# Block inverses of the gated DeltaNet mixer: from ten steps over pairs of heads to five steps over fours

## Chip, core and metric

The kernel runs on one core of a Trainium2 chip. The metric is device time in microseconds (us) of one execution. The kernel before takes 1231.0 us, the median of three runs (1230.87 to 1231.64).

## What is computed

A decoder trunk of two layers over 512 tokens of width 1024, all in float32. Layer 0 mixes tokens with gated linear attention, layer 1 with a gated DeltaNet; each is followed by a gated ConvFFN, and each sublayer by a LayerNorm. The change lies in the DeltaNet of layer 1, which has 8 heads:

```python
m = jnp.where(strict, jnp.einsum('bhnik,bhnjk->bhnij', k_beta, k) * decay_ij, 0.0)
rhs = jnp.concatenate([v * beta[..., None], k_beta * jnp.exp(bcum)[..., None]], axis=-1)
sol = lax.linalg.triangular_solve(m, rhs, left_side=True, lower=True, unit_diagonal=True)
...
def step(state, inp):
    qk_n, u_n, w_n, qd_n, kd_n, cd_n = inp
    v_new = u_n - jnp.einsum('bhck,bhkv->bhcv', w_n, state)
    o_n = jnp.einsum('bhck,bhkv->bhcv', qd_n, state) + jnp.einsum('bhij,bhjv->bhiv', qk_n, v_new)
    state = state * cd_n[..., None, None] + jnp.einsum('bhck,bhcv->bhkv', kd_n, v_new)
    return state, o_n
```

The kernel works on blocks of 128 tokens, so each head has four 128x128 unit lower triangular matrices, and it forms their inverses instead of solving.

## The kernel before

**The large work.** Almost all of the program is projections: 128x512 matmuls of float32 split in a high and a low part (xh, xl against wh, wl), three products each. In the DeltaNet (`gdn`) they come as 24 column projections `fm` of 24 such matmuls (k, v, q of eight heads), then as the gate projection `tm` (192 of them), then the output projection. A list of tasks (Python generators) is run beside them: `pump`, called after every few large matmuls, resumes each task whose due time on a rough clock (`clk`) has come. That only sets the order in which the program is written; the scheduler beneath may move an instruction ahead of others that wait for data, and every engine then executes its queue in the order that results.

**The inverses.** VectorE inverts the 32x32 diagonal blocks of all heads at once (`base`). They pass through DRAM (`dinv`, `dinvt`) and come back by small DMAs on the queues of SP and GpSimd into `T` (transposed inverses, one tile for a pair of heads) and `rm` (the result, one tile for a head). TensorE then joins blocks, 32 to 64 (`quarter`) and 64 to 128 (`half`). Each join has two products: V = A·T into one PSUM bank, copied to SBUF, then R = T'·V, copied into `rm`; `am` is A. In `quarter` both 64-blocks of a matrix are joined, the products being 32x32: V at rows 0-31 and output partitions 32-63 (n=0) and at rows 64-95 and 96-127 (n=1), R at rows 32-63 and 0-31 and at rows 96-127 and 64-95; one more product, R at rows 32-63 and 32-63, gives the transposed block that the half join needs, copied into `T`. So there are five places in TensorE's array, five tiles of it. In `half` the products are 64x64, V at rows 0-63 and partitions 64-127, R at rows 64-127 and 0-63: two tiles. A pair of heads has eight matrices, so one join of a pair has 8 products at each place. Every float32 product is executed as two passes, and the trace counts passes.

`inverses` goes over pairs: step `quarter(k)` writes the V products of pair k beside the R products of pair k-1, and `half(k)` likewise. Ten steps; `block_turn` holds them `INV_APART` = 3.2 us of that rough clock apart, and the first comes `INV_DELAY` = 18 after the first pair's DMAs are issued:

```python
for step, k in ((quarter, 0), (quarter, 1), (quarter, 2), (half, 0), (quarter, 3), (half, 1), (quarter, 4),
                (half, 2), (half, 3), (half, 4)):
    yield from self.block_turn(INV_APART)
    step(k)
```

`block_turn` also ties the first product of a step behind the last 128x512 matmul written before it (`behind`), so a step does not start earlier.

**What follows.** `chain(g)` runs the recurrence of heads 4g to 4g+3 over the four blocks of tokens, 128x128 products named vn, kT, qs, s, o, ks, with `tm` matmuls between; it needs `rm` of its four heads. q's last two heads have transposes qT and products pq, which are among the steps too. After the chains the gates are applied, transposed (yT), and the output projection follows.

Of the kernel before, what the change touches and what calls it, by code (L numbers as in the profile page):

```python
# [46 lines left out]
LOOKAHEAD = 2  # L47
TAIL = 4
HEADSTART = 4
INV_DELAY = 18.0  # L50
INV_APART = 3.2
CONV_DELAY = 6.0
V_DELAY = 18.0
COLS_DELAY = 64.0
# [8 lines left out]
def c4(t):  # L63
    return t.rearrange("p (c i) -> p c i", c=4)


def blk(i, n=P):
    return slice(i * n, i * n + n)


class Trunk:
# [1386 lines left out]
    def gdn(self, li, g, b):  # L1458
        nc = self.nc
# [11 lines left out]
        q, k, v, am, rm, pj = ([None] * DH for _ in range(6))  # L1471
# [131 lines left out]
        def base():  # L1603
# [17 lines left out]
            for pair in range(4):  # L1621
                t = self.slot("T")
                t8 = t.rearrange("p (u i) -> p u i", u=8)
                nc.gpsimd.memset(t8[:32, :, 32:], 0.0)
                for hd in (2 * pair, 2 * pair + 1):
                    rm[hd] = self.slot("rm")
                    nc.gpsimd.memset(rm[hd], 0.0)
                for qq in range(4):
                    rw = blk(qq, 32)
                    u = pair // 2 * 64 + qq * 16 + pair % 2 * 8  # L1630
                    if qq < 3:
                        nc.sync.dma_start(t8[rw, :, blk(qq % 2, 32)],
                                          self.dinvt[u:u + 8].rearrange("u i c -> i u c"))
# [11 lines left out]
        parts = []  # L1645

        def inverses():

            low, up = slice(0, 32), slice(32, 64)
            units = [(i, ck, 4 * i + ck) for i in range(2) for ck in range(4)]
            views = {}

            def views_of(pair):
                if pair not in views:
                    both = (2 * pair, 2 * pair + 1)
                    views[pair] = ([c4(am[hd]) for hd in both], [c4(rm[hd]) for hd in both], parts[pair], self.slot("V"))
                return views[pair]

            def quarter(k):
                if k < 4:
                    a, _, t8, vs = views_of(k)
                    pv = [self.psum("V") for _ in range(2)]
                if k > 0:
                    _, r, t0, v0 = views_of(k - 1)
                    pr = [self.psum("R") for _ in range(2)]
                for i, ck, u in units:
                    w = blk(u, 32)
                    for n, o in ((0, 0), (1, 64)):  # L1670
                        m = slice(o + 32, o + 64)
                        if k < 4:
                            self.mm(pv[n][m, w], a[i][o:o + 32, ck, m], t8[o:o + 32, u, low])
                        if k > 0:
                            self.mm(pr[n][o:o + 32, w], v0[m, w], r[i][m, ck, m])
                    if k > 0:
                        self.mm(pr[0][up, w], r[i][up, ck, up], v0[up, w])
                if k < 4:
                    nc.scalar.copy(vs[up, :256], pv[0][up, :256])
                    nc.vector.tensor_copy(vs[96:, :256], pv[1][96:, :256])  # L1680
                if k > 0:
                    nc.scalar.copy(t0[up, :, low], pr[0][up, :256].rearrange("p (u i) -> p u i", u=8))
                    for n, o in enumerate((0, 64)):
                        for i in range(2):
                            nc.vector.tensor_copy(r[i][o:o + 32, :, o + 32:o + 64],
                                                  pr[n][o:o + 32, blk(i)].rearrange("p (c i) -> p c i", c=4))

            def half(k):
                if k < 4:
                    a, _, t8, vs = views_of(k)  # L1690
                    pv = self.psum("V")
                if k > 0:
                    _, r, _, v0 = views_of(k - 1)
                    pr = self.psum("R")
                for i, ck, u in units:
                    w = blk(u, 64)
                    if k < 4:
# [3 lines left out]
                if k < 4:  # L1701
                    nc.scalar.copy(vs[64:, :], pv[64:, :])
                if k > 0:
                    for i in range(2):
                        nc.vector.tensor_copy(r[i][:64, :, 64:], pr[:64, blk(i, 256)].rearrange("p (c i) -> p c i", c=4))
                        am[2 * k - 2 + i] = None
                        self.set(("rm", 2 * k - 2 + i), 1.0)
# [229 lines left out]
```

## Time and profile before

| | before |
|---|---|
| runs, median (lowest to highest) | 1231.0 us (1230.87 to 1231.64) |
| the profiled execution | 1231.2 us |
| its span, first to last instruction | 1229.5 us |
| granted TensorE clock | 0.999 |
| steps of the inverses on TensorE | 719.8 to 755.0 us of the span |
| V and R products, passes | 192 of V, 256 of R (320 of 32x32, 128 of 64x64) |

The profile comes from one execution. PE is TensorE, DVE VectorE, ACT ScalarE, POOL GpSimd, and SP issues most DMAs. The chain of waits follows the program back from its last instruction to whatever released each step, so its rows add up to the span; in the timeline a row is a run of like instructions with its start, its length and its count, and a TensorE row's length holds the last matmul's own latency, so that rows overlap by it.

### The profile page before, as it was taken

What the parts mean: (1) busy time and instruction counts of PE and PEld (TensorE: products, weight loads), DVE (VectorE), ACT (ScalarE), POOL (GpSimd) and SP (SyncE); (2) the same over time, 40 slices, a digit from 0 to 9 for tenths busy, and PEclk for the clock granted to TensorE, in tenths of its full rate; (3) what the DMA queues carried; (4) which work ended last, traced back from release to release, by engine and by line L of the source; (5) the groups of instructions that cost most, each with busy time, mean ns of one, the idle gap of its engine ahead of it and who ended that gap; (6) DMA issues with size and microseconds to landing.
All of it is one profiled execution on the core that took longest, in us unless ns stands there. A gap on an engine that the chain in (4) does not pass through costs nothing.

```text
span 1229.5 us, 17177 instructions
## 1 busy us (share of the span) xinstructions
PE 1218.9 (99%) x6546; PEld 1028.8 (84%) x6546; DVE 933.8 (76%) x1533; ACT 605.6 (49%) x1068; POOL 122.6 (10%) x159
## 2 busy tenths in 40 slices
PE   9999999999999999999999999999999999999997
PEld 8888888988888888888988888988988888888886
DVE  4966986689957895666779975688589966796667
ACT  5644764544434443454678555644644434443440
POOL 4000000081000000001152030200053000000000
PEclk9999999999999999999999999999999999999999
DMA  7332353442453123333344351234352263223311
GB/s 213 112 103 69 87 173 101 148 127 72 136 152 99 56 66 113 113 105 104 102 131 129 101 135 37 85 122 138 120 154 69 73 201 89 88 81 103 110 62 69
DMA packets 171042, 133.67 MB, mean 109 GB/s; under 512 B 16374, under 2 KB 140090, under 8 KB 170960
## 3 DMA queue, kind: packets, MB, share of 16 engines
q1 hardware_dynamic: 165888, 123.62, 33.8%
q0 software_dynamic: 3872, 8.30, 2.2%
q8 instruction: 51, 0.84, 0.3%
q10 hardware_dynamic: 1200, 0.66, 0.2%
q14 instruction: 31, 0.25, 0.1%
HBM read 126.77 MB, written 5.78 MB: 108 GB/s over the span
## 4 chain that ended last, share of the span: by engine, by line
PE 96%; DVE 2%; DMA 1%; issue 0%; ACT 0%; DVEq 0%; SPq 0%; ACTq 0%
PE fm L203 54%; PE tm L203 20%; PE fold L203 13%; PE o L203 1%; PE xT L220 1%; PE pq L203 1%; PE pg L203 1%; PE vn L203 1%; PE V L203 0%; PE yT L220 0%; PE s L203 0%; PE qs L203 0%; PE ks L203 0%; DVE wl L649 0%; DMA h<-in_x_dram 0%
## 5 line engine op out<-in xcount | busy, mean ns | idle before, releaser
L203 PE MATMUL fm<-xh,wh 128*128 128x512 f32 (+2 forms) x1104 | 401.8, 366 | 0.7 <-ACT xh L649 0.7
L203 PE MATMUL fm<-xl,wh 128*128 128x512 f32 (+2 forms) x1104 | 399.9, 365 | 0.0
L203 PE MATMUL fm<-xh,wl 128*128 128x512 f32 (+1 forms) x1080 | 392.8, 366 | 0.0
L649 DVE TENSOR_TENSOR wl<-raw,wh 128x1024 fp32r<-128x1024 f32 (+1 forms) x162 | 201.0, 1243 | 152.5 <-ACT wh L649 151.9
L649 ACT CAST wh<-raw 128x1024 fp32r<-128x1024 f32 (+1 forms) x163 | 169.2, 1040 | 224.3 <-PE fm L203 142.1
L203 PEld LDWEIGHTS fm<-xh,wh 128*128 128x128 f32 (+1 forms) x1104 | 206.9, 188 | 33.8 <-ACT xh L649 0.9
L203 PEld LDWEIGHTS fm<-xl,wh 128*128 128x128 f32 (+1 forms) x1104 | 207.0, 188 | 32.5
L203 PEld LDWEIGHTS fm<-xh,wl 128*128 128x128 f32 x1080 | 202.8, 189 | 33.0
L922 DVE SCALAR_TENSOR_TENSOR conv<-fm,ffn_cw,conv 128x511 f32<-128x511 f32 x112 | 83.5, 746 | 8.4 <-ACT conv L920 7.0
L203 PE MATMUL fold<-wh,fh 128*128 128x512 f32 x224 | 87.7, 391 | 0.0
L203 PE MATMUL fold<-wl,fh 128*128 128x512 f32 x224 | 87.4, 390 | 0.1
L203 PE MATMUL fold<-wh,fl 128*128 128x512 f32 x224 | 87.2, 389 | 0.0
L649 ACT CAST wh<-b 128x1024 fp32r<-128x1024 f32 x48 | 49.7, 1055 | 60.3 <-PE fold L203 25.7
L940 ACT ACTIVATE conv<-conv 128x512 f32<-128x512 f32 x44 | 27.9, 634 | 80.4 <-DVE conv L922 80.4
L849 POOL TENSOR_TENSOR h<-h,gb 128x512 f32<-128x512 f32 x16 | 27.4, 1738 | 335.4 <-DMA gb<-in_ln_g_dram 229.6
L649 DVE TENSOR_TENSOR wl<-b,wh 128x1024 fp32r<-128x1024 f32 x48 | 58.0, 1224 | 2.3 <-ACT wh L649 2.3
L1453 DVE SCALAR_TENSOR_TENSOR conv<-fm,gdn_cw,conv 128x511 f32<-128x511 f32 (+2 forms) x72 | 54.0, 790 | 3.2 <-ACT conv L1451 2.6
L203 PE MATMUL tm<-wh,xh 128*128 128x512 f32 x128 | 52.9, 414 | 0.0
L203 PEld LDWEIGHTS fold<-wh,fh 128*128 128x128 f32 x224 | 42.0, 188 | 9.9 <-DVE h L1011 1.2
L203 PE MATMUL tm<-wh,xl 128*128 128x512 f32 x128 | 50.2, 392 | 0.0
L203 PE MATMUL tm<-wl,xh 128*128 128x512 f32 x128 | 50.1, 391 | 0.0
L203 PEld LDWEIGHTS fold<-wl,fh 128*128 128x128 f32 x224 | 42.0, 188 | 9.4 <-DVE wl L649 0.9
(348 smaller groups left out, 1960.3 us busy)
## 6 DMA issues: line engine op xcount, KB each, us to landing
raw<-in_ffn_w_in_dram SPq DMA_DIRECT2D x88, 512.0 KB, 3.9
raw<-in_gdn_w_in_dram SPq DMA_DIRECT2D x32, 512.0 KB, 4.1
raw<-in_ffn_w_out_dram SPq DMA_DIRECT2D x28, 512.0 KB, 3.7
raw<-in_gla_w_in_dram SPq DMA_DIRECT2D x26, 512.0 KB, 3.6
b<-in_ffn_w_out_dram SPq DMA_DIRECT2D x24, 512.0 KB, 4.8
raw<-in_gla_w_out_dram SPq DMA_DIRECT2D x8, 512.0 KB, 4.0
raw<-in_gdn_w_out_dram SPq DMA_DIRECT2D x8, 512.0 KB, 3.9
h<-in_x_dram SPq DMA_DIRECT2D x8, 256.0 KB, 4.3
```

The costliest lines, as they stand in the source:

```text
L203: t = self.nc.tensor.matmul(out, a, b, start=start, stop=stop, skip_group_check=joined)
L220: t = self.nc.tensor.transpose(out, a, self.ident[:n, :n])
L649: return self.nc.scalar.copy(dst_h, src), self.nc.vector.tensor_sub(dst_l, src, dst_h)
L849: nc.gpsimd.tensor_mul(h[hf], h[hf], gb[hf])
L922: nc.vector.scalar_tensor_tensor(a[:, d:], ps[:, :S - d], tap(2 - d), a[:, d:], ALU.mult, ALU.add)
L940: nc.scalar.activation(a, a, AF.Gelu)
L1453: self.conv = nc.vector.scalar_tensor_tensor(a[:, d:], ps[:, :S - d], tap(3 - d), a[:, d:], ALU.mult, ALU.add)
```

## The change

The pairs become fours. `quarter(k)` writes the V products of four k beside the R products of four k-1, and the same in `half`, so there are three calls of each, twice as large; the second bank of V and R that `quarter` already had is filled to 512 columns, and `half` takes two banks for each. The copies out of PSUM double with them. `quarter(2)` and `half(0)` share a step, so five steps are left; they stand 5.4 apart on the rough clock, the first at 20.0 after the DMAs.

```diff
-INV_DELAY = 18.0
-INV_APART = 3.2
+INV_DELAY = 20.0
+INV_APART = 5.4
...
-            units = [(i, ck, 4 * i + ck) for i in range(2) for ck in range(4)]
+            units = [(i, ck, 4 * i + ck) for i in range(4) for ck in range(4)]
...
             def quarter(k):
-                if k < 4:
-                    a, _, t8, vs = views_of(k)
+                if k < 2:
+                    a, _, t, (vs, _) = views_of(k)
                     pv = [self.psum("V") for _ in range(2)]
...
                     for n, o in ((0, 0), (1, 64)):
                         m = slice(o + 32, o + 64)
-                        if k < 4:
-                            self.mm(pv[n][m, w], a[i][o:o + 32, ck, m], t8[o:o + 32, u, low])
+                        if k < 2:
+                            self.mm(pv[n][m, w], a[i][o:o + 32, ck, m], t[i // 2][o:o + 32, u % 8, low])
...
-                if k < 4:
-                    nc.scalar.copy(vs[up, :256], pv[0][up, :256])
-                    nc.vector.tensor_copy(vs[96:, :256], pv[1][96:, :256])
+                if k < 2:
+                    nc.scalar.copy(vs[up, :], pv[0][up, :])
+                    nc.vector.tensor_copy(vs[96:, :], pv[1][96:, :])
...
                 for i, ck, u in units:
-                    w = blk(u, 64)
-                    if k < 4:
-                        self.mm(pv[64:, w], a[i][:64, ck, 64:], t8[:64, u, :])
+                    n, w = u // 8, blk(u % 8, 64)
+                    if k < 2:
+                        self.mm(pv[n][64:, w], a[i][:64, ck, 64:], t[n][:64, u % 8, :])
                     if k > 0:
-                        self.mm(pr[:64, w], v0[64:, w], r[i][64:, ck, 64:])
...
+                        self.mm(pr[n][:64, w], v0[n][64:, w], r[i][64:, ck, 64:])
...
-            for step, k in ((quarter, 0), (quarter, 1), (quarter, 2), (half, 0), (quarter, 3), (half, 1), (quarter, 4),
-                            (half, 2), (half, 3), (half, 4)):
+            for steps in (((quarter, 0),), ((quarter, 1),), ((quarter, 2), (half, 0)), ((half, 1),), ((half, 2),)):
                 yield from self.block_turn(INV_APART)
-                step(k)
+                for step, k in steps:
+                    step(k)
                 yield 0.1
```

What the scheduler makes of it on TensorE is not the five steps as written. In the rows below V_ and R_ are PSUM banks, T_6237, T_6291, T_6363 and T_6417 the inverses of pairs 0 to 3, am and rm the matrices of single heads, and a row stands for one product or for as many as its x says.

First place: TensorE where the inverses begin. Before, the step ends after the products of pair 0 on its two places:

```order
L203 MATMUL V_6447<-T_6237,am_5205 32x32
L203 MATMUL V_6448<-T_6237,am_5205 32x32
L220 MATMUL qT_6467<-ident_86,conv_6308 128x128 x4
L220 MATMUL qT_6476<-ident_86,conv_6392 128x128 x4
L203 MATMUL pq_6485<-conv_6308,conv_5282 128x128 x4
L203 MATMUL pq_6491<-conv_6392,conv_5319 128x128 x4
```

Now the products of pair 1 follow, one place after the other:

```order
L203 MATMUL V_6467<-T_6237,am_5205 32x32
L203 MATMUL V_6468<-T_6237,am_5205 32x32
L203 MATMUL V_6467<-T_6291,am_5255 32x32 x4
L203 MATMUL V_6467<-T_6291,am_5264 32x32 x4
L220 MATMUL qT_6503<-ident_86,conv_6308 128x128 x4
L220 MATMUL qT_6512<-ident_86,conv_6392 128x128 x4
L203 MATMUL pq_6521<-conv_6308,conv_5282 128x128 x2
L203 MATMUL V_6468<-T_6291,am_5255 32x32 x4
L203 MATMUL V_6468<-T_6291,am_5264 32x32 x4
L203 MATMUL pq_6521<-conv_6308,conv_5282 128x128 x2
```

The V products of the second bank for pair 1 have moved between the pq products; the first step is entered twice.

Second place: TensorE in the second step. Before, the five places take turns:

```order
L203 MATMUL V_6517<-T_6291,am_5255 32x32
L203 MATMUL R_6519<-rm_6239,V_6446 32x32
L203 MATMUL V_6518<-T_6291,am_5255 32x32
L203 MATMUL R_6520<-rm_6239,V_6446 32x32
L203 MATMUL R_6519<-V_6446,rm_6239 32x32
```

Now three places take turns eight times, then two (seven times, for heads 2 and 3), then the other two eight times, then one alone; the V products of pair 3 are not in this step at all:

```order
L203 MATMUL V_6541<-T_6363,am_5410 32x32
L203 MATMUL R_6543<-rm_6239,V_6465 32x32
L203 MATMUL R_6543<-V_6465,rm_6239 32x32
...
L203 MATMUL R_6543<-rm_6293,V_6465 32x32
L203 MATMUL R_6543<-V_6465,rm_6293 32x32
...
L203 MATMUL V_6542<-T_6363,am_5410 32x32
L203 MATMUL R_6544<-rm_6239,V_6465 32x32
...
L203 MATMUL R_6544<-rm_6293,V_6465 32x32 x4
L203 MATMUL R_6544<-rm_6295,V_6465 32x32 x3
```

What was written as one turn of five places has been pulled apart into four stretches.

Third place: TensorE in the 64x64 products. Before, V and R of a step take turns between large matmuls:

```order
L203 MATMUL tm_6655<-wh_6400,xl 128x512
L203 MATMUL V_6728<-T_6291,am_5255 64x64
L203 MATMUL R_6729<-rm_6239,V_6446 64x64
L203 MATMUL V_6728<-T_6291,am_5264 64x64
L203 MATMUL R_6729<-rm_6241,V_6446 64x64
L220 MATMUL qT_6749<-ident_86,conv_6497 128x128 x4
```

Now, from the last 32x32 products on (R_6644 is the second bank of the R products of the second four, V_6703 and V_6704 the V products of the first four, V_6729 and V_6730 those of the second, R_6731 and R_6732 the R products of the first):

```order
L203 MATMUL V_6542<-T_6417,am_5595 32x32 x4
L203 MATMUL R_6643<-V_6539,rm_6421 32x32
L203 MATMUL fm_6458<-xl,wh_6316 128x512
L203 MATMUL fm_6458<-xh,wl_6317 128x512
L203 MATMUL R_6644<-rm_6365,V_6539 32x32 x4
...
L203 MATMUL V_6703<-T_6237,am_5196 64x64 x4
...
L203 MATMUL V_6729<-T_6363,am_5419 64x64 x4
L203 MATMUL R_6731<-rm_6239,V_6465 64x64 x4
L203 MATMUL R_6731<-rm_6241,V_6465 64x64 x4
L203 MATMUL V_6730<-T_6417,am_5586 64x64
L203 MATMUL R_6732<-rm_6293,V_6466 64x64
```

24 V products stand in a row, then 8 R products in a row, and only the last 8 of each take turns. The steps three and four have grown together; two large matmuls separate them from the products before.

Counted over the whole stretch, TensorE goes to the small products ten times before (one step each) and seven times now:

| | products in their order, per place (R' is the extra R product) | behind it |
|---|---|---|
| A | V on two places by turns, 8 each; then V on one place, 8 | 8 qT, 2 pq |
| B | V on one place, 8 | 6 pq, 6 fm |
| C | V, R, R' by turns, 8 each; R, R' by turns, 7 and 6; V, R on the other places by turns, 8 each; R alone, 7; R' 2, R 1 each | 6 fm |
| D | V on one place, 8 | 4 fm |
| E | R, R' by turns, 16 and 15; V on one place, 8; R' 1 | 2 fm |
| F | R on one place, 16; then 64x64: V 24, R 8, V and R by turns, 8 each | 6 tm, 4 vn, 4 kT |
| G | 64x64: R 16 | 6 tm |

Before, the ten visits have in their order: V by turns on two places, 8 each; all five places by turns, 8 each; three places by turns, about 6 each, two by turns, about 5, then all five for the rest (the third visit); 64x64 V 8; five places by turns, 8 each; 64x64 V and R by turns, 8 each; R and R' on three places by turns, 8 each; 64x64 V and R by turns, 8 each, twice; 64x64 R 8. The queues of SP and GpSimd issue the DMAs of T and rm in the same order as before. Behind the seventh visit the program holds the same instructions as before, with chain 0 and chain 1 begun earlier among the `tm` matmuls: 42 `tm` now stand between the last o product of the chains and the first yT, and before it was 12.

More of the change, by code (lines that the diff above doesn't have):

```diff
@@ L1651, in inverses, with views_of @@
             low, up = slice(0, 32), slice(32, 64)
-            units = [(i, ck, 4 * i + ck) for i in range(2) for ck in range(4)]
+            units = [(i, ck, 4 * i + ck) for i in range(4) for ck in range(4)]
             views = {}
[L1655 to L1659, printed above, removed]
+            def views_of(four):
+                if four not in views:
+                    heads = range(4 * four, 4 * four + 4)
+                    views[four] = ([c4(am[hd]) for hd in heads], [c4(rm[hd]) for hd in heads],
+                                   parts[2 * four:2 * four + 2], [self.slot("V") for _ in range(2)])
+                return views[four]
             def quarter(k):
-                if k < 4:
-                    a, _, t8, vs = views_of(k)
+                if k < 2:
+                    a, _, t, (vs, _) = views_of(k)
                     pv = [self.psum("V") for _ in range(2)]
                 if k > 0:
-                    _, r, t0, v0 = views_of(k - 1)
+                    _, r, t0, (v0, _) = views_of(k - 1)
                     pr = [self.psum("R") for _ in range(2)]
@@ L1677, in quarter @@
                         self.mm(pr[0][up, w], r[i][up, ck, up], v0[up, w])
-                if k < 4:
-                    nc.scalar.copy(vs[up, :256], pv[0][up, :256])
-                    nc.vector.tensor_copy(vs[96:, :256], pv[1][96:, :256])
+                if k < 2:
+                    nc.scalar.copy(vs[up, :], pv[0][up, :])
+                    nc.vector.tensor_copy(vs[96:, :], pv[1][96:, :])
                 if k > 0:
-                    nc.scalar.copy(t0[up, :, low], pr[0][up, :256].rearrange("p (u i) -> p u i", u=8))
+                    for i in range(2):
+                        nc.scalar.copy(t0[i][up, :, low],
+                                       pr[0][up, blk(i, 256)].rearrange("p (u i) -> p u i", u=8))
                     for n, o in enumerate((0, 64)):
-                        for i in range(2):
+                        for i in range(4):
                             nc.vector.tensor_copy(r[i][o:o + 32, :, o + 32:o + 64],
@@ L1688, in half @@
             def half(k):
[L1689 to L1691 removed]
+                if k < 2:
+                    a, _, t, vs = views_of(k)
+                    pv = [self.psum("V") for _ in range(2)]
                 if k > 0:
                     _, r, _, v0 = views_of(k - 1)
[L1694 removed]
+                    pr = [self.psum("R") for _ in range(2)]
                 for i, ck, u in units:
[L1696 to L1698 removed]
+                    n, w = u // 8, blk(u % 8, 64)
+                    if k < 2:
+                        self.mm(pv[n][64:, w], a[i][:64, ck, 64:], t[n][:64, u % 8, :])
                     if k > 0:
[L1700 to L1702 removed]
+                        self.mm(pr[n][:64, w], v0[n][64:, w], r[i][64:, ck, 64:])
+                if k < 2:
+                    nc.scalar.copy(vs[0][64:, :], pv[0][64:, :])
+                    nc.scalar.copy(vs[1][64:, :], pv[1][64:, :])
                 if k > 0:
[L1704 to L1707, printed above, removed]
[L1709 to L1710 removed]
+                    for i in range(4):
+                        nc.vector.tensor_copy(r[i][:64, :, 64:],
+                                              pr[i // 2][:64, blk(i % 2, 256)].rearrange("p (c i) -> p c i", c=4))
+                        am[4 * k - 4 + i] = None
+                        self.set(("rm", 4 * k - 4 + i), 1.0)
+            for steps in (((quarter, 0),), ((quarter, 1),), ((quarter, 2), (half, 0)), ((half, 1),), ((half, 2),)):
                 yield from self.block_turn(INV_APART)
[L1712 removed]
+                for step, k in steps:
+                    step(k)
                 yield 0.1
```

## The prediction, made before the changed kernel was run

> **What bounds the kernel now.** I read the busy times first, then what TensorE waited for, then the chain of waits through the stretch that is changed, then the timeline of TensorE inside the visits.
>
> ```profile
> PE 1218.9 (99%) x6546; PEld 1028.8 (84%) x6546; DVE 933.8 (76%) x1533; ACT 605.6 (49%) x1068; POOL 122.6 (10%) x159
> PEclk9999999999999999999999999999999999999999
> PE 96%; DVE 2%; DMA 1%; issue 0%; ACT 0%; DVEq 0%; SPq 0%; ACTq 0%
> PE warm L723 <- POOL one L97: 1.1, 1, 1.1
> ```
>
> TensorE (PE) is busy for 99% of the span at full clock, 96% of the chain is its own work, and its longest wait anywhere is 1.1 us, at the start. So nothing is to be had by letting something else finish sooner. The time changes only by what TensorE itself spends on the small products, and by waits that come in or go.
>
> Here is the chain of waits through the ten visits (start, length, what; the rows are laid end to end, so their lengths add up):
>
> ```profile
> 719.84 0.79 PE V L203 x31
> 720.63 1.02 PE qT L220 x8
> ...
> 723.44 1.38 PE fm L203 x6
> 725.70 1.58 PE fm L203 x6
> 728.30 1.58 PE fm L203 x6
> 729.89 1.07 PE V L203 x16
> 730.96 1.59 PE fm L203 x6
> 732.55 1.36 PE tm L203 x6
> 734.79 1.58 PE tm L203 x6
> 737.45 0.59 PE qT L220 x4
> 738.31 0.65 PE qT L220 x4
> ...
> 742.14 0.63 PE R L203 x48
> 742.77 2.72 PE tm L203 x11
> 746.57 1.59 PE tm L203 x6
> ...
> 749.05 0.44 PE kT L220 x4
> 750.56 1.59 PE tm L203 x6
> ...
> 753.94 1.07 PE R L203 x16
> 755.01 1.58 PE tm L203 x6
> ```
>
> A visit is either a row of its own or the hole between two rows: the second reaches from 723.44+1.38 = 724.82 to 725.70, 0.88 us. The ten take 0.79, 0.88, 1.02, 1.07, 0.88, 1.08, 0.63, 1.08, 1.07 and 1.07, together 9.57. The six large matmuls behind one take 1.58 or 1.59 instead of the 1.36 to 1.38 that six take elsewhere, and eight qT 1.02 where the row below has 0.87: a price for coming back of 0.15 to 0.22 each time, 1.95 in all. The ten visits cost 11.52 us.
>
> What fills a visit is seen in the timeline of TensorE, in the third visit (32x32) and the sixth (64x64); start, length, what:
>
> ```profile
> 727.27 0.19 PE L203 MATMUL V<-T,am 32*32 32x32 f32 x1
> 727.27 0.19 PE L203 MATMUL R<-rm,V 32*32 32x32 f32 x1
> 727.28 0.19 PE L203 MATMUL R<-V,rm 32*32 32x32 f32 x1
> ...
> 727.49 0.19 PE L203 MATMUL V<-T,am 32*32 32x32 f32 x1
> ...
> 736.41 0.22 PE L203 MATMUL V<-T,am 64*64 64x64 f32 x1
> 736.41 0.22 PE L203 MATMUL R<-rm,V 64*64 64x64 f32 x1
> ...
> 737.16 0.22 PE L203 MATMUL V<-T,am 64*64 64x64 f32 x1
> ```
>
> Passes at different places start together, within 0.01 us; the next pass at the same place starts one round later. From 727.27 to 727.49 lie seven rounds, 0.0315 us each; from 736.41 to 737.16 thirteen, 0.058 each. So a visit is paid by rounds, not by passes: its price is the number of passes that the busiest place has to take one after the other. That a lone place gains nothing is in the chain: the fourth visit has V alone and the sixth V and R by turns, twice the passes, and they took 1.07 and 1.08.
>
> Places that do not stand by turns do not share rounds. The third visit shows it: its turns of three places, then two, then five make 12+10+6 = 28 rounds, 0.88 us by the rate above, and it took 1.02; the second, with the same 80 passes in turns of five, has 16 rounds and took 0.88, the seventh with 16 rounds 0.63.
>
> **The sum.** Before there are 16+16+28+16+16 = 92 rounds of 32x32 and 5 x 16 = 80 of 64x64: 92 x 0.0315 + 80 x 0.058 = 2.90 + 4.64 = 7.54 us. The other 3.98 of the 11.52 is the price of ten visits, 0.40 each, entry and return included.
>
> In the changed order a product again has two passes, and each stretch counts the products of its busiest place twice. A: 16 for the turns and 16 for V alone. B: 16. C: 16, 14, 16, 14 and 4 for the rest. D: 16. E: 32, 16 and 2. F: 32, and then in 64x64 48 for V, 16 for R, 16 by turns. G: 32. That is 32+16+64+16+50+32 = 210 rounds of 32x32 and 80+32 = 112 of 64x64: 6.62 + 6.50 = 13.12 us. Seven visits add 7 x 0.40 = 2.79. Inside F the array goes from 32x32 to 64x64, which no row before shows; between nothing and a whole visit's 0.40 I take 0.14, what a lone 64x64 visit has beside its rounds (1.07 less 16 x 0.058). Together 16.05, so **the small products cost 4.5 us more**: 5.6 for lost turns, less 1.05 for three visits fewer and the switch in F.
>
> What else moves. Two waits of TensorE lie in the stretch before:
>
> ```profile
> 707.63 0.87 PE qT L220 x8
> ...
> 803.34 1.36 PE yT L220 x12
> 804.71 0.30 PE yT L220
> 805.01 0.24 PE tm L203
> 805.81 21.28 PE tm L203 x93
> 827.09 1.75 PE yT L220 x16
> ```
>
> The eight qT of the last pair ran from 737.45 to 738.96, 1.51 us with one tm between; eight in a row take 0.87, a tm 0.23 (21.28 for 93), the return 0.15, so 0.26 was waiting. Sixteen yT with two tm ran from 803.34 to 805.81, 2.47, where 1.75 + 0.46 were due: 0.26 again. In the new order the qT stand some 10 us behind their data and the yT behind 42 tm instead of 12; I count both as gone, -0.5.
>
> A new wait comes between E and F. F's first R products read what VectorE copies from E's last V products, and only two large matmuls lie between.
>
> ```profile
> L1680 DVE COPY V<-V x4: 429/430/430, 720.7 to 735.5; 32x256 f32<-32x256 f32 x4
> L1685 DVE COPY rm<-R x16: 267/277/290, 726.3 to 744.0; 32x128 f32<-32x128 f32 x16
> L649 DVE TENSOR_TENSOR wl<-raw,wh 128x1024 fp32r<-128x1024 f32 (+1 forms) x162 | 201.0, 1243 | 152.5 <-ACT wh L649 151.9
> ```
>
> 32x128 took 0.28 and 32x256 0.43, so the copy, now 32x512, takes by extension 0.74. With the last pass's 0.19 and the 0.07 that lay between the end of V (719.77 + 0.86, 720.63) and its copy (720.7) it is done some 1.05 us after the last V pass starts; two large matmuls with the change back and forth take 0.78. I count +0.26; it is nothing if TensorE's return is slower, and 1.2 more if a weight split of VectorE (wl) should stand ahead of it, but the order has none there. The other doubled copies have 64x64 products or six large matmuls over them: ScalarE's 64x512 copy of V has 16 rounds of other V and more, the copies into rm ahead of chain 0 have six tm.
>
> The DMAs keep their issue order. The first visit comes later, by one more group of six fm (1.36), so T of pair 0 is there. The latest is the last part of pair 3's T:
>
> ```profile
> 729.24 1.17 SPq L1632 DMA_DIRECT2D T<-dinvt  x2
> DMA to landing us min/median/max: 1.8/2.1/3.7
> ```
>
> Its second issue starts at about 729.7 and lands at 731.8, at worst 733.4. It is wanted by the V products at the end of E. By the charges above, E's V comes near 734.4 (721.2 for A's start, 1.3 for A, 1.5 qT and pq, 0.8 B, 2.8 pq and fm, 2.3 C, 1.6 fm, 0.8 D, 1.1 fm, 1.0 of E): no wait. The chains begin earlier, chain 0 near 743 instead of 748, which gains nothing while TensorE has no wait to lose.
>
> Sum: +4.5 - 0.5 + 0.26 = +4.3 on the profiled execution's 1231.2 (1.7 of it outside the span), 1235.5; the median of the runs lies 0.2 lower, so **1235.3 us**.
>
> The unseen price is that of a round with one place of 32x32 alone: 112 of the 210 are such (A 16, B 16, C 14, D 16, E 18, F 32). By the nearest rows it lies between 0.007, the distance of passes at different places, and 0.058, the lone place of 64x64; I take 0.0315, since the 64x64 rows show a lone place at the same rate as two. The ends give -2.8 and +3.0 us.
>
> **Rivals.** (1) The engine overlaps stretches that are written one after the other. Then only the busiest place of a visit counts: 32+16+32+16+32+32 = 160 rounds, and 64+32 = 96: 5.04 + 5.57 + 2.79 + 0.14 = 13.5, which is +2.0, and with the waits 1232.8. [...] Against it stands the third visit, which took 0.14 more than the second with the same passes. Chance 0.12.
>
> (2) A visit has a fixed price, whatever it holds: ten of about 1.15 us (0.79 to 1.29) look like that. Then seven cost 8.1 instead of 11.5, and with the waits the time is 1227.3, faster than before. It decides once a round costs under a quarter of what I read (5.6 us of lost rounds against 1.05 + 0.26 gained). Against it: the starts within a visit are evenly spaced from first to last, and the 64x64 visits leave no room after their sixteenth round. Chance 0.07.
>
> (3) More waits than I count: V and R products now stand where one copy holds up a whole four. Two copies late by one wl of VectorE each would be +2.5, 1237.8. For it: VectorE is 76% busy; against: the order has no such row ahead of the copies. Chance 0.13.
>
> **Numbers.** My forecast, 1233.5 to 1237, has 0.68. The range goes from 1232.0 to 1238.3, which takes in (1), (3) and both ends of the lone round. A measurement tells about 0.2% (2.5 us) from no change. Faster: 0.07, rival 2. Within: 0.16, rival 1 and the edge of mine. Slower: 0.77.
>
> **What would show it.** Visit C should take near 2.3 us before its fm and F near 6.0; the V passes of F should be 0.058 apart for 48 passes, with R only after them. Seven visits, some 16 us in all; vn near 743 us; no wait at the last qT and at yT; a span near 1233.7. I am wrong if C takes 1.3 (stretches overlap), if F takes under 3 (fixed price), or if TensorE shows a wait of over 1 us between 721 and 747.

## The result and the profile after

The changed kernel takes 1238.54 us, the median of six runs, against 1231.15 us before on the same chip: a ratio of 1.0049, with a 95% interval of 1.0038 to 1.006. The direction was foretold, but the median lies 3.2 us above the forecast of 1235.3, outside the 1233.5 to 1237 that had 0.68 of the chance, and 0.2 above the top of the whole range. The six runs do not gather round their median, and their mean granted clock goes with the time:

| run | 1 | 2 | 3 | 4 | 5 | 6 |
|---|---|---|---|---|---|---|
| us | 1239.05 | 1239.26 | 1238.03 | 1234.79 | 1239.31 | 1234.34 |
| mean granted clock | 0.994 | 0.994 | 0.996 | 0.998 | 0.995 | 0.998 |

The first is the profiled one. Its busy times, from the profile's page:

```profile
span 1237.4 us, 17154 instructions
...
PE 1227.3 (99%) x6546; PEld 1038.6 (84%) x6546; DVE 932.8 (75%) x1531; ACT 603.9 (49%) x1066; POOL 124.0 (10%) x159
```

TensorE has as many passes as before, 6546, and is 8.4 us longer busy. The whole span's list of what TensorE waited for has two rows, neither of them in the inverses:

```profile
PE warm L723 <- POOL one L97: 1.1, 1, 1.1
PE fm L203 <- ACT xh L649: 0.7, 1, 0.7
```

So the time is in TensorE's own work. The chain of waits through the seven visits, A to G (start, length, what):

```profile
721.34 1.12 PE V L203 x48
722.47 1.02 PE qT L220 x8
723.49 0.45 PE pq L203 x4
723.93 0.62 PE V L203 x16
724.55 1.53 PE pq L203 x12
726.09 1.38 PE fm L203 x6
...
729.52 1.59 PE fm L203 x6
731.11 0.62 PE V L203 x16
731.72 1.12 PE fm L203 x4
732.84 1.03 PE R L203 x57
...
734.43 0.69 DVE V L1681
...
735.16 1.19 PE R L203 x32
736.36 4.73 PE V L203 x45
...
744.45 2.72 PE tm L203 x6
747.17 0.89 PE vn L203 x8
...
748.49 2.00 PE R L203 x32
750.50 1.59 PE tm L203 x6
```

Two rows are out of scale. In F, 45 V passes of 64x64 take 4.73 us, 0.105 each, where G's 32 passes take 2.00, 0.0625 each; and the six tm behind F take 2.72, where the six behind G take 1.59. The same stretch, cut into pieces of 3.41 us (a third of the 10.24 us for which the clock is down), shows why (length, TensorE's busy time and passes, granted clock, DMA share, GB/s):

```profile
733.22:736.63 3.41, 3.28 (x104) 1.00 0.79 292
736.63:740.04 3.41, 3.41 (x36) 0.50 0.17 20
740.04:743.46 3.42, 3.42 (x51) 0.50 0.39 138
743.46:746.87 3.41, 3.41 (x22) 0.50 0.00 0
746.87:750.28 3.41, 3.41 (x45) 1.00 0.00 0
```

From 736.63 to 746.87 us, three of these pieces, **the clock granted to TensorE was 0.50, half of full, while it was busy all the time**. In the profile of before the granted clock is 1.00 from 719 to 755 us and 0.999 in the mean. In the 40 slices of the page, 31 us each, the halving does not show.

### The profile page after: what moved, and what is told of

Read it like the earlier page. It is cut to its first block, busy times and chain, and to the rows that moved or that the text cites. A ratio compares the mean times of both kernels' runs of the same rounds, so it can differ in the third digit from the quotient of the medians.

```text
span 1237.4 us, 17154 instructions
## 1 busy us (share of the span) xinstructions
PE 1227.3 (99%) x6546; PEld 1038.6 (84%) x6546; DVE 932.8 (75%) x1531; ACT 603.9 (49%) x1066; POOL 124.0 (10%) x159
## 4 chain that ended last, share of the span: by engine, by line
PE 98%; DVE 1%; ACT 0%; issue 0%; DVEq 0%; POOL 0%; ACTq 0%; POOLq 0%
PE fm L203 54%; PE tm L203 20%; PE fold L203 15%; PE o L203 2%; PE xT L220 1%; PE V L203 1%; PE R L203 1%; PE pq L203 1%; PE vn L203 1%; PE pg L203 1%; PE yT L220 1%; PE qs L203 0%; PE s L203 0%; PE ks L203 0%; PE ds L203 0%; PE sa L203 0%
```

## What was tried

Two things had to be told apart: what the new order costs at a full clock (the prediction's sum), and what halves the clock. The texts on record name their theories as they stood at the time.

**1. The turns by themselves.** Two kernels with the pairs of before, written order kept by force. The first keeps the turns of V and R, the second writes all V of a step and then all R; nothing else differs.

```diff
                 yield from self.block_turn(INV_APART)
+                self.pin = True
                 step(k)
+                self.pin = False
```

```diff
-                        if k > 0:
-                            self.mm(pr[n][o:o + 32, w], v0[m, w], r[i][m, ck, m])
-                    if k > 0:
-                        self.mm(pr[0][up, w], r[i][up, ck, up], v0[up, w])
+                for i, ck, u in units if k > 0 else ():
...
-                    if k > 0:
-                        self.mm(pr[:64, w], v0[64:, w], r[i][64:, ck, 64:])
+                for i, ck, u in units if k > 0 else ():
```

> The kernel before with the products of a step pinned to the order in which they are written. Only the third visit changes: its five places take turns throughout (16 rounds instead of 28), but a large matmul group is split by two products. Theory: -0.4 for rounds, +0.3 for the extra visit, 1230.5 to 1231.5 us; it is the base for the next kernel.

> As the last one, but each step writes all its V products first and then all its R products: 48 rounds of 32x32 and 48 of 64x64 more, the same products, the same visits, no visit longer than 2.1 us, so no clock change. Theory (stretches written one after the other share no rounds): 48 x 0.0315 + 48 x 0.058 = +4.3 us over the kernel with turns, 1235 to 1236. Rivals (the engine overlaps places whatever the order, or a visit has a fixed price): no change, 1231 to 1232.

Measured: 1231.48 us with turns (ratio 1.0002, 0.9993 to 1.001; 11 runs) and 1234.17 without (1.0024, 1.0015 to 1.0032; 11 runs). The loss of turns costs 2.7 us without any other part of the change; by the prediction's count it should be 4.3. The chain shows where most of the rest is. Sixth visit with turns, V in the rows shown and R between them:

```profile
736.75 0.20 PE V L203
...
737.77 0.05 PE V L203
737.83 0.59 PE qT L220 x4
```

and without turns:

```profile
737.13 0.90 PE V L203 x13
738.03 0.06 PE R L203
...
738.21 0.75 PE R L203 x13
738.96 0.59 PE qT L220 x4
```

1.08 against 1.83 us: sixteen lost rounds of 0.058 would be 0.93, and 0.75 came, since V's last three passes and R's first three stand beside each other in between. So these 64x64 stretches of different places overlapped by about three rounds (0.18 us), not wholly. In 32x32 the lost turns cost less than their rounds: the second visit takes 0.88 us with turns (724.96 to 725.84) and 1.11 without (724.63 to 725.74), 0.23 more where sixteen rounds of 0.0315 would be 0.50. The 1.11 is about what 32 rounds (1.01) and the entry (0.1) come to, so it is the turns of five places that cost more than 16 rounds. The rows of before hinted at it: the second and the seventh visit both have 16 rounds by the prediction's count, on five and on three places, and took 0.88 and 0.63.

**2. The price of a lone round.** The kernel before, with the first half step's V computed three times, then eight times: 32 and 112 rounds of one 64x64 place more.

```diff
+                if k == 0:
+                    self.pin = True
+                    for _ in range(2):
+                        for i, ck, u in units:
+                            w = blk(u, 64)
+                            self.mm(pv[64:, w], a[i][:64, ck, 64:], t8[:64, u, :])
+                    self.pin = False
```

> The kernel before, with the eight 64x64 V products of its first half step computed three times over (the same values to the same place): a stretch of 48 rounds at one place, 2.9 us, with large matmuls on both sides. Theory (the clock is halved after a window of about 3.4 us, on a grid of its own, that holds next to no large matmul): 32 rounds x 0.058 = +1.9 us, 1233.2, clock as before, no halved stretch. Rival (any lone place lowers the clock): a halved stretch, 1235 or more.

> The same with the eight V products computed eight times over: 128 rounds at one place, 7.4 us without a large matmul, longer than two windows of 3.4, so that one window lies wholly in it wherever the grid falls. Theory: 112 x 0.058 = +6.5 us at full clock (1237.8), and in every run a halved stretch of 6.8 or 10.2 us on top, which costs half its length, 1241 to 1243. Rival (the halving in the changed kernel has another cause, as its DMAs or its copies): 1237.8, full clock.

Measured: 1233.3 us (1.0017, 1.0008 to 1.0027) and 1237.38 (1237.12 to 1238.02, all four at a clock of 0.998 or 0.999). The rows of the chain, of the first kernel and of the second:

```profile
730.02 2.94 PE V L203 x48
```

```profile
729.59 7.60 PE V L203 x128
```

2.94 - 1.07 for 32 rounds is 0.058 each: the round's price holds, and a visit has no fixed price. The second kernel also took down the theory of that day, that 3.4 us without a large matmul halve the clock: 7.60 us is longer than two pieces of 3.41, so one lies wholly in it wherever the pieces begin. This piece of it has nothing but lone 64x64 passes, and behind it the clock stays at 1.00:

```profile
731.28:734.69 3.41, 3.41 (x62) 1.00 0.89 301
```

**3. The changed kernel, its third step split or its order altered.** First with `quarter(2)` and `half(0)` as two steps; then with steps 4.4 apart from 24.0 on, once in written order by force and once left to the scheduler, which restores most of the turns.

```diff
-            for steps in (((quarter, 0),), ((quarter, 1),), ((quarter, 2), (half, 0)), ((half, 1),), ((half, 2),)):
+            for steps in (((quarter, 0),), ((quarter, 1),), ((quarter, 2),), ((half, 0),), ((half, 1),), ((half, 2),)):
```

> The changed kernel with its third step written as two, so that six tm stand behind the last 32x32 products and eighteen between the first 64x64 V products and the next step; in the order the 64x64 V and R then take turns again (64 rounds where the changed kernel has 80). Theory (the clock is halved because some 6 us go by with next to no large matmul): no run below a clock of 0.998, no halved stretch in the profile, runs within 0.6 us of each other; the small products cost 16.1 by the prediction's prices, less 0.9 for 16 rounds, plus 0.8 for two more visits, so 1234 to 1235.5 us. Rival (small products at one place halve the clock wherever they stand, or it is chance): runs scatter by 4 us as those of the changed kernel did, median 1237 to 1239.

> The changed kernel with the products of a step pinned to the order in which they are written, and the steps at 24.0 and 4.4 of the rough clock so that T of the last pair has landed. V and R take turns: 96 rounds of 32x32 and 96 of 64x64, in eight visits (two of them of one product). Theory (lost turns cost 118 x 0.0315 + 32 x 0.058): 3.0 + 5.6 + 8 x 0.4 = 11.8 us for the small products against 11.5 before, full clock throughout: 1231 to 1232. Rival (fours as such cost, by their longer copies and waits, or the clock falls anyway): 1234 or more.

> The changed kernel with its first step at 24.0 and its steps 4.4 apart on the rough clock, and nothing pinned: the order now has most turns (128 rounds of 32x32, 108 of 64x64) in six visits, since T of the last pair is due before the second step. Theory by the prediction's prices: 4.0 + 6.3 + 6 x 0.4 + 0.1 = 12.8 us against 11.5, 1232 to 1233; its longest stretch without a large matmul, the fourth visit, is some 3.6 us, so a halving now and then. Rival (the delay makes the chains late and uncovers a wait at the end of the gates): over 1234 at full clock, with a wait of TensorE ahead of yT.

Measured: the split 1235.3 us (1235.04 to 1236.71; 1.0035, 1.0023 to 1.0048; two of its five runs, at a clock of 0.997, lie 1.4 above the others, at 0.999, which its theory had ruled out), the forced turns 1233.28 (1232.04 to 1235.64; 1.0018, 1.0009 to 1.0027), the scheduler's turns 1236.0 (1.0032, 1.002 to 1.0044). The last fall into two groups: runs at a clock of 0.998 or 0.999 lie at 1231.97 to 1233.56, those at 0.994 to 0.996 at 1235.3 to 1238.23. The forced turns spread likewise, from 1232.04 at 0.999 to 1235.64 at 0.996, where 1231 to 1232 was expected. So most of the turns restored bring the full-clock time near that of before, and a lower clock comes back in some executions all the same. Both kernels were profiled in an execution that kept its clock, so where they lose it was not seen. In the split kernel it came in the profiled execution, for one piece only, in which six tm stood right behind the 32x32 passes:

```profile
736.38 2.52 PE tm L203 x6
738.90 2.59 PE V L203 x32
```

```profile
733.32:736.73 3.41, 3.28 (x96) 1.00 0.32 118
736.73:740.14 3.41, 3.41 (x18) 0.50 0.15 16
740.14:743.56 3.42, 3.42 (x32) 1.00 0.39 142
```

**4. Idle large matmuls, behind the 32x32 passes and among them.** The changed kernel with six 128x512 matmuls whose output nobody reads, first ahead of the 64x64 V of either four, then instead ahead of the second bank's 32x32 R in F, that is in the middle of the lone passes:

```diff
+                if k == 2:
+                    ps = self.psum("fill")
+                    self.pin = True
+                    for c in range(6):
+                        self.mm(ps, self.xh[:, c, :P], self.xh[:, c, :])
+                    for i, ck, u in units:
+                        self.mm(pr[1][64:96, blk(u, 32)], v0[96:, blk(u, 32)], r[i][96:, ck, 96:])
+                        self.pin = False
```

> The changed kernel with six 128x512 matmuls of no use ahead of the 64x64 V products of the first four and six more ahead of those of the second, 2.7 us of work, and one visit more. Theory: the changed kernel at full clock would take 1234.5; with the added work 1237.7, and since the large matmuls end a halving after one window at most (3.4 us, up to 1.7 us lost) 1237.7 to 1239.4, no halved stretch over 3.5 us: work added and next to nothing lost. Rival (the halving does not hang on large matmuls): 1238.5 + 3.2 = 1241.7.

> The changed kernel with six idle 128x512 products put into its sixth visit ahead of the second bank's 32x32 products of R, that is into the middle of the lone-place stretch and not behind it. The six products themselves cost about 1.4 us, the visit split in two about 0.4 us, and the wait for VectorE's copy is covered by them. Theory 1 (that stretch, from the tail of the fifth visit over the lone 32x32 rounds to the first 64x64 rounds, is what falls into a quiet 3.41 us): no run is halved, all clocks are 0.998 or more, all runs lie within 0.6 us of each other at about 1235.1 us (1234.55 unhalved + 1.4 + 0.4 - 0.26 for the covered wait - 0.9 for the filled gaps and turns). Theory 2 (it makes no difference where the idle products stand; the quiet stretch lies elsewhere): runs scatter over about 4 us, from 1235 to 1241 us, with clocks from 0.994 to 0.999, as with the idle products behind the stretch.

Measured: behind, 1236.89, 1237.42, 1241.85 and 1241.92 us, the first two at a clock of 0.998 and 0.999, the last two at 0.994. So the idle matmuls behind did not cap the loss at one piece (up to 1.7 us), as its theory had it: the halved runs are 4.4 to 5.0 us longer. None of these was profiled. Among, five runs within 0.43 us, **1235.35 us** (1235.3 to 1235.73), every clock 0.998 or 0.999, with more work than the changed kernel, and 3.2 us below its median (0.6 to 1.0 above its two whole-clock runs). Its chain:

```profile
734.28 1.59 PE fill L203 x6
735.87 1.12 PE R L203 x32
736.99 2.00 PE V L203 x32
```

Now 32 V passes after the switch take 2.00, as in G. The scheduler also moved the two fm: the six idle matmuls stand in their place, and the fm come only behind these 32 V passes, at 738.99. So, by these five runs, the stretch behind which the clock falls is the one that this cut in two: the end of E, two fm, VectorE's copy and F's 32x32 R. Since the idle matmuls also cover the wait for the copy, 0.13 us, the two are not told apart here.

**5. A lone 32x32 place without any wait.** The kernel before, its first visit prolonged by 240 rounds of one 32x32 place:

```diff
+                if k == 0:
+                    self.pin = True
+                    for _ in range(15):
+                        for i, ck, u in units:
+                            self.mm(pv[0][up, blk(u, 32)], a[i][low, ck, up], t8[low, u, low])
+                    self.pin = False
```

> The kernel before with the products of its first quarter step for one of the two mixers' V repeated: 120 extra 32x32 products, all at the same one of the five places, that is 240 rounds of one place more (the repeats write what the product has written). By 0.0315 us a round this is 7.56 us more: 1238.9 us at a full clock. Theory 1 (the clock is halved when a whole stretch of 3.41 us sees little of the array used, and a lone 32x32 place is little): every run is halved, the profile shows the halved stretch in or right behind these rounds, and the time is 1242 to 1244 us. Theory 2 (TensorE's waits, not its small products, make the chip halve the clock): the extra rounds are busy without a gap, so 1238.9 us at a granted clock of 0.998 or more.

Measured: 1242.89 us (1242.85 to 1242.92; 1.0095, 1.0079 to 1.011), all four at 0.994. The pieces of its span, the long row of V reaching from 719.75 to 730.62:

```profile
720.99:724.40 3.41, 3.41 (x113) 1.00 0.35 51
724.40:727.81 3.41, 3.41 (x70) 0.50 0.34 58
...
731.23:734.64 3.41, 3.41 (x18) 0.50 0.88 299
734.64:738.05 3.41, 3.41 (x95) 1.00 0.04 13
```

The first piece that holds nothing but these passes, 720.99 to 724.40, is busy from end to end, and the clock is halved right behind it. It comes back after a piece of 128x128 products, at 734.64. So TensorE need not wait for its clock to be halved; the theory that its waits alone do it has fallen.

**6. Several 32x32 places at once.** Does the clock fall behind 32x32 products at any number of places, or only behind a lone place? First 600 extra products at five places by turns; then 32 products with 512 columns of data at the four places on the diagonal by turns.

```diff
+                            for n, o in ((0, 0), (1, 64)):
+                                m = slice(o + 32, o + 64)
+                                self.mm(pv[n][m, w], a[i][o:o + 32, ck, m], t8[o:o + 32, u, low])
+                                self.mm(pd[n][o:o + 32, w], a[i][m, ck, m], a[i][m, ck, m])
+                            self.mm(pd[0][up, w], a[i][up, ck, up], a[i][up, ck, up])
```

> As the kernel with 240 extra rounds of one 32x32 place, but the extra products go to all five places by turns, so that up to five of them run side by side. Theory 1 (the share of the array in use counts): five places are more than the lone 64x64 place that left the clock whole for 7.6 us, so no halving, a granted clock of 0.998 or more, and, if a place's round still takes 0.0315 us times the number of rounds over the number of places that overlap, a time between 1232.8 us (all five overlap) and 1238.9 us (none does). Rival (products in 32x32 pieces never count as use, whatever their number): halved as the lone place is, a clock of 0.996 or less and at least 3 us above what its own extra TensorE time explains.

```diff
+                    for c in range(8):
+                        for o in range(0, P, 32):
+                            m = slice(o, o + 32)
+                            self.mm(ps[m], am[c % 2][m, m], am[c % 2][m, :])
```

> The kernel before with 32 idle products in its first 32x32 visit, each of 32 rows, 32 columns of weights and 512 columns of data, at the four places on the diagonal by turns: few and long instructions, so that TensorE cannot run out of them as it did with 600 short ones. Two passes of 128 columns took 0.22 us in the transposes, so one product takes about 0.9 us, eight to a place: 7.0 us if the four places run side by side, 28 us if one at a time. Theory 1 (the share of the array in use counts, a quarter is enough, as a lone 64x64 place was): with the four side by side nothing is halved, granted clock 0.998 or more, 1238.2 us. Rival (32x32 pieces never count as use): halved behind the first 3.41 us of these products, clock 0.996 or less, and the time is 3 us or more above that of the products at a full clock.

The first gave 1267.46 us (1266.07 to 1268.48), far outside what either theory expected, and does not answer the question: the list of TensorE's waits has two rows of nothing that the profile could name,

```profile
PE D L203 <- issue: 15.0, 6, 3.5
PE V L203 <- issue: 6.1, 3, 2.1
```

and the pieces show that it was mostly idle in the piece ahead of the halving (busy for 1.17 of 3.42 us):

```profile
720.93:724.35 3.42, 1.17 (x139) 1.00 0.31 48
724.35:727.76 3.41, 0.55 (x51) 0.50 0.32 51
```

The second is clearer. Its products filled most of one piece and all of the next, and the clock stayed whole; later a wait of 1.85 us ("issue") left another piece half empty (busy for 1.56 of 3.41 us), and right behind it the clock was 0.50:

```profile
720.50:723.91 3.41, 3.41 (x64) 1.00 0.41 61
723.91:727.32 3.41, 3.41 (x40) 1.00 0.43 68
734.15:737.56 3.41, 1.56 (x83) 1.00 0.16 61
737.56:740.98 3.42, 3.42 (x16) 0.50 0.03 7
```

Its 1242.28 us (1239.28 to 1243.06), not 1238.2, are then the products, 6.6 for 60 of the 64 passes, that wait, and a halved piece at another place. Sixty passes in 6.62 us are 0.44 for a round of four, so the places ran side by side (expected: 7.0 us for all if they do, 28 if not). In the profiled executions, then, the clock stayed at 1.00 behind four 32x32 places side by side, as it did behind one 64x64 place (2). Behind one 32x32 place (5) it was 0.50, and so it was behind a piece that was mostly idle. Two things stay open. These passes are also sixteen times as long as those of experiment 5, and the length was not varied by itself, though the data at one place go through at nearly the same rate: 32 columns in 0.030 us there (113 passes in 3.41), 512 in 0.44 here. And the four runs lie between a clock of 0.995 and 0.998; only one was profiled.

**What stood ahead of the half clock.** The stretches at 0.50 in the visits or right behind them lasted 3.41 us in the split kernel, 3.42 in the kernel with the 32 wide products, 10.24 in the changed kernel and in experiment 5, and 34.13 in the kernel with 600 extra products: 1, 1, 3, 3 and 10 pieces of 3.41. The piece right ahead of such a stretch held lone 32x32 passes throughout (5), or over half of it was waiting and most of the rest 32x32 passes (6, busy for 1.17 and 1.56 us), or, in the changed kernel, it was a mixture: 2.4 of 3.41 us in 32x32 passes at one place or two (733.22 to 734.43, 735.16 to 736.36) and a wait of 0.13, beside two fm and the first 64x64 passes. The DMA traffic does not go with it: the piece ahead of the halving moved 292 GB/s in the changed kernel, but one of the kernel with 112 extra rounds (2) moved 301 and the clock stayed at 1.00 behind it, and the pieces ahead of the halvings of experiments 5 and 6 moved 48 to 61. In the two kernels with most turns restored (3) the 32x32 R products stand mostly by turns on two or three places, and TensorE stands idle for about half a microsecond soon after (0.60 and 0.46 us, "issue"); which of these, if either, lowers their clock is not shown. Counted back from the halvings in steps of 3.41 us, an edge lies at 720.50, 720.93 and 720.99 us of the span in the three kernels of 5 and 6, not at one time for all. By that I read the two groups of runs, as an estimate: the 32x32 work of E and F, some 2.8 us, is nearly as long as a piece, and in some executions an edge divides it. This reading was not tested by itself, nor how long such a stretch has to be, nor whether the part of the array in use matters; the profile has one execution of each kernel.

## Why the prediction was right, and where not

**Bound: right at a full clock.** TensorE has no new wait of its own in the list, and the time moved by what it spends on small products. But the prediction knew only two ways for the time to move, TensorE's small products and its waits; the clock is a third.

**The rounds: right, a little too dear.** Each visit of the profiled execution with its return, worked out of the chain as it was before:

| | A | B | C | D | E and the wait | F | G |
|---|---|---|---|---|---|---|---|
| by the prediction's terms | 1.41 | 0.90 | 2.42 | 0.90 | 2.24 | 6.19 | 2.26 |
| measured | 1.28 | 0.81 | 2.26 | 0.83 | 1.87 | 10.65 | 2.23 |

C, with its four stretches, took 2.26 us (a hole of 2.05, 0.21 more for the fm behind) against the 2.3 said, and not the 1.3 that would have been the sign of overlap. All but F together are 0.85 below their terms. B and D, one stretch each, are 0.16 of it, so a visit costs a little less than 0.40; for the rest, experiment 1 has two causes (64x64 stretches overlap by some rounds, and lost turns of 32x32 cost less than their rounds), and E's wait was shorter than its 0.26. The shares were not separated. The lone 32x32 round, the unseen price, was 0.0315 us as near as can be read: D's 16 passes take 0.62 and F's 32 take 1.12 in the last kernel of experiment 4, 0.031 for each more. The switch from 32x32 to 64x64, taken as 0.14, is the 2.00 us of the 32 V passes in experiment 4 less 32 x 0.058 = 1.86.

**The waits: right.** The last qT take 0.87 and the yT 1.75 for sixteen, so both waits of before are gone:

```profile
753.88 0.87 PE qT L220 x8
```

The new wait on VectorE's copy is there, but small: TensorE was idle for 0.13 us of the piece that holds it (3.28 of 3.41), where 0.26 was counted. The copy's row in the timeline, with the time VectorE stood idle ahead of it:

```profile
734.41 0.70 DVE L1681 COPY V<-V 32x512 f32<-32x512 f32 x1 [2.90 <-PE V L203]
```

It starts at 734.41, right behind E's V, which was put near 734.4 and began at 733.74, and it takes 0.70, where 0.74 was taken. The weight split did not stand ahead of it.

**The step that failed is F's 80 rounds of 64x64 at 0.058 us each, a price that holds at a full clock, which the prediction took for granted.** F was to take near 6.0 us. It took 9.29 up to its tm and 1.36 more in them, because the clock was halved from its first 64x64 passes until shortly before the end of its tm (0.50 from 736.63 to 746.87 us). At a full clock F would be, by estimate, its 1.19 for R, 80 x 0.058 = 4.64 and 0.22 for the return, 6.05; that puts the sum at 15.3 us of visits, +3.8, less 0.5 for the waits: +3.3, or 1234.5 us. The two runs at a clock of 0.998 gave 1234.34 and 1234.79. The other 4.6 us of the profiled execution are the halved clock. So of the 7.4 us by which the median rose, the prediction's mechanism gives 3.2 to 3.6 (the two runs at 0.998 against 1231.15), and the rest comes from a cause for which it has no term. That the median misses the range by only 0.2 is luck: the upper end was set for a lone round of 0.058 and for late copies, and neither came. In the profiled execution vn came at 747.17 instead of near 743, and the span is 1237.4 instead of 1233.7. The page of before showed a clock of 0.9 or more in all 40 slices, and its trace 1.00 through the visits; that the new order puts some 2.8 us of 32x32 work at one place or two close together, E's 1.59 and the 1.19 at F's start, could be read off the order; that the clock is halved behind it could not, since no visit of before is longer than 1.08 us.

**The rivals.** Overlap of whole stretches (1) is refuted: 2.7 us for the turns alone, where full overlap would have cost nothing. The fixed price (2) too: G with 32 passes cost 2.23, B with 16 (of 32x32) cost 0.81, and 32 more rounds of 64x64 in one visit cost 1.87. More waits (3) would have given a time near the measured one, 1237.8, for the wrong reason: the list of waits has none.

## What to carry to other kernels

Count small products on TensorE by the rounds of the busiest place, stretch by stretch, and keep different places by turns: batching them by operand loses that, 2.7 us in experiment 1. Then look at how long TensorE would do little but 32x32 passes at one place or two: here some 2.8 us of it, with two large matmuls between, was followed by half the clock for 10.24 us in the changed kernel and for 3.41 in the split one, and only in some executions (a mean clock of 0.994 to 0.996 in four runs of six, 0.997 in two of five). With six idle 128x512 matmuls in the middle of the stretch the clock was 0.998 or 0.999 in five of five runs; with six behind it, 0.994 in two of four. Where the times of one kernel fall into groups, compare the mean granted clock run by run before looking for waits.

## What was not expected of the hardware

- A TensorE that was busy for 3.41 of 3.41 us with passes at one 32x32 place was at a clock of 0.50 next (experiment 5); with one 64x64 place for 7.60 us (experiment 2), or with longer passes at four 32x32 places for 6.62 (experiment 6), it stayed at 1.00.
- Once halved, the clock came back, in these profiles, only after a piece with work on the whole array (128x128 or 128x512) in it, though not after every such piece (experiment 5: 727.81 to 731.23 held 0.6 us of qT): one piece in the split kernel (tm at once) and in the kernel with the wide products (fm), three in experiment 5, three in the changed kernel, where two held only 64x64 passes, and ten (34.13 us, busy for 0.55 to 1.61 us of a piece where the extra products ran) in the kernel with 600 extra products.
- TensorE stood still nine times in that kernel, for 1.8 to 3.5 us and mostly 2.1, with about 128 short passes between, and nothing that the profile names as the cause: 1200 extra passes took 36 us, 0.030 each. What limits it was not tried.
